# A decoder layer on one core: squares of the inverse square root on ScalarE, narrower shuffles, block sums by additions, masks and decays on GpSimd

## The chip, the core and the metric

The kernel runs on one core of a Trainium2 chip. The metric is the time of one execution on the device in microseconds (us). In the profile, TensorE is PE (PEld for its weight loads), VectorE is DVE, ScalarE is ACT, GpSimd is POOL, and SyncE, which issues the DMAs, is SP.

## What is computed

One decoder layer for a prompt (16 meta tokens and 256 tokens) and eight sample sequences of four tokens: 304 columns in all, 288 once the meta tokens are dropped. The width is 2048. Cut to what matters, the reference is:

```python
z = rms_norm(x, norm_mix) @ w_in
o_a, S_a = rwkv7_mixer(z[..., :RWKV_COLS], ...)   # 16 heads of 64, a recurrence over tokens
o_b, S_b = retention_mixer(z[..., RWKV_COLS:], ...)   # 4 heads of 256, in chunks
h = x + concat(o_a, o_b) @ w_out
hn = rms_norm(h, norm_ffn)
h = h + (silu(hn @ w_gate) * (hn @ w_up)) @ w_down
y = rms_norm(h, norm_final)
```

The places that need 1/sqrt are the three RMS norms, the length of the RWKV keys (`kk / max(sqrt(sum(kk*kk)), 1e-12)`), the group norm behind the RWKV heads, and the RMS norm behind the retention heads. The RWKV recurrence is computed in units of 64 tokens; inside a unit a triangular system has to be inverted.

## The kernel before

**Weights and projections.** All weights come from HBM in one packed stream, in the order in which they are used. `cast` (line 617) has ACT round 512 columns to a short float format (`wh`), and `rest` (line 629) has DVE compute what was cut off (`wl`). Each projection tile is three matmuls per 128 rows of depth (`xh` by `wh`, `xl` by `wh`, `xh` by `wl`) that add into a PSUM bank called `acc`; there are two of these banks. `main` (line 634) issues them one after the other: first 59 tiles of the input projection, in the order of `ORDER` (p: the three tiles k, r, v of a pair of RWKV heads; r: the six tiles q, k, v of a retention head; g: its two gate tiles), then the output projection in two halves, then the FFN.

**Streams.** Everything else runs beside this as generators, called streams: `constants`, `lora_post`, `lora_weights`, `pair` with `by_token`, `inverse`, `units`, `sample`, `bonus` and `pair_out` for each of the eight pairs of heads, and `ret` for each of the four retention heads. A stream issues some instructions for any of the engines and then yields. Its matmuls use six PSUM banks called `mm`.

**The order.** PE runs its instructions strictly in the order of the program, and so does each other engine. The order is found by a planner before the program is made. `Plan.book` (line 348) gives every instruction a price from its engine, its operation and its width, and keeps a clock for each engine, so that the draft knows when each stream's step would be ready. `Plan.pick` (line 426) looks at PE's clock: as long as a stream's step is ready by then, that step is issued, and otherwise the next projection matmul. The draft's choices are then repeated when the real program is made. The prices that bear on this change are, in `book`:

```python
dur, tail = {"stream_shuffle": (148, 90), ...}.get(what, (62 + per * n + 67 * each, 83))
dur, tail = (60 + 0.85 * n, 60) if what == "memset" else (185 + 0.8 * n, 60) if what == "tensor_copy" else (265 + 2 * n, 60)
```

The second line is GpSimd's: 265 + 2 n ns for a product or sum of n columns. An instruction that needs the result of the one before it on the same engine is started `tail` plus 30 ns after that one's duration. The draft also notes how long each tile lives, and `Room` lays the tiles out in one arena from that; in the profile they are all called `arena_dt.float` or `arena_dt.float32r`. A wrapper (line 302) issues every instruction, so all of them carry that line, and a group is known by its shape and tile.

**The pieces that are touched.** `rsqrt` (line 705) computes 1/sqrt on DVE: a scale and an added epsilon (or a floor), a shift and a subtraction of the bits for a first guess, and two corrections, each with two products and an addition. It is called with 304 columns in `constants`, with 312 and a floor in `pair`, with 288 in `pair_out` and in `ret`, and with 3 columns in `rstd_from`, which serves the last two norms. `lora_weights` (line 870) loads two small weight tiles for a pair, twice per pair, and splits them into `hi` (ACT) and `lo` (DVE); in the second call ACT then copies a part of `lo` into `hi`. `inverse` (line 1095) inverts the triangular system: it multiplies `mt` by a mask, sums four 16-column blocks of it into `rr` by a reduction, sends 15 rows of `rr` to all rows of their block by stream shuffles on DVE, in three groups of five, and lets GpSimd do 15 steps of a multiply and an add each on 15 - s columns of five units (75 columns in step 0, 5 in step 14). Then DVE makes two masked copies of `mt`, called `em`, masks the result, transposes it, spreads it over blocks, and PE multiplies. `sample` (line 1219) runs the sample sequences of a pair; it decays the state `s0` by `d4` before it adds what the new tokens bring.

Of the kernel before, what the change touches and what calls it, by code (L numbers as in the profile page):

```python
# [15 lines left out]
P = 128  # L16
# [290 lines left out]
class Plan:  # L307
# [40 lines left out]
    def book(self, eng, what, a, k):  # L348
# [14 lines left out]
        if eng == "PE":  # L363
            done = self.array(what, *a[:3], at) + 170
        elif eng == "SP":
            self.clock[eng] = at = max(self.clock[eng] + 400, at)
            self.dma = max(self.dma, at + 1400) + 4 * out.shape[0] * n / 320
            done = self.dma + 600
        else:
            part = out.shape[0] < P  # L370
            each = sum(math.prod(x.shape[1:]) == 1 for x in ins) if n > 1 else 0
            if eng == "DVE":
                big = max(math.prod(x.shape[1:]) for x in aps)
                per = 0.56 if what == "tensor_scalar" and ins[0].name not in self.banks else 1.05
                dur, tail = {"stream_shuffle": (148, 90), "transpose": (95 + 1.02 * n, 80), "tensor_reduce": (40 + 1.8 * big, 85),
                             "tensor_tensor_scan": (65 + 2.1 * n, 85)}.get(what, (62 + per * n + 67 * each, 83))
            elif eng == "ACT":
                dur, tail = 108 + 0.83 * n + 90 * each - 40 * (ins[0].name in self.banks), 94
            else:
                dur, tail = (60 + 0.85 * n, 60) if what == "memset" else (185 + 0.8 * n, 60) if what == "tensor_copy" else (265 + 2 * n, 60)  # L380
# [158 lines left out]
class Step:  # L539
# [165 lines left out]
    def rsqrt(self, src, scale, eps, floor=None, out=None):  # L705


        dve = self.dve
# [3 lines left out]
        a = self.t([m, n], "rsa")  # L712
        if floor is not None:
            dve.tensor_scalar(x, src, floor, None, op0=ALU.max)
        else:
# [17 lines left out]
    def start(self):  # L733
# [3 lines left out]
        self.dve.memset(self.ones, 1.0)  # L737
        xh, xl = self.xh, self.xl
# [131 lines left out]
    def lora_weights(self, p, half, z):  # L870
# [12 lines left out]
        dve.tensor_sub(lo, lw, hi)  # L883
# [211 lines left out]
    def inverse(self, mt):  # L1095
# [13 lines left out]
        ems = []  # L1109
# [109 lines left out]
    def sample(self, p, v, ax, axd, bs, d4, s0):  # L1219
# [60 lines left out]
        dve.tensor_mul(s0, s0, d4.to_broadcast([P, NB, 64]))  # L1280
# [489 lines left out]
```

## Time and profile before

| | us |
|---|---|
| median of 3 runs | 1557.36 |
| lowest and highest | 1556.4 and 1557.76 |
| the profiled execution | 1558.99 |
| its span, first to last instruction | 1557.1 |
| busy: ACT wh<-wr, 826 casts | 501.6 |
| busy: DVE wl<-wr,wh, 826 subtractions | 563.3 |
| busy: POOL products and sums, 240 | 94.5 |

A row of a group gives line, engine, operation, the tile written and those read, the shape and the count; then the busy time and the mean of one in ns; then the engine's idle time ahead of these instructions and who ended it. A row of a stretch gives the start and end, the length, the busy time and count of PE, PEld, DVE, ACT and POOL, then the granted clock of TensorE, the share of DMA time and GB/s. A row of the order in time gives start, length, engine and operation; neighbours of one operation are merged under the shape of the first, and in brackets stands the idle time before and who ended it. The span and the device time differ by the work around the program, 1.9 us in this execution.

### The profile page before, as it was taken

Reading aid. Unit: us, or ns where it says so; the run is one execution under the profiler, and the core shown is the slowest. Engines: PE = TensorE matmul, PEld = TensorE weight load, DVE = VectorE, ACT = ScalarE, POOL = GpSimd, SP = SyncE. Lnnn points to the kernel's source line nnn. Section 1 sums busy time; section 2 is a strip of 40 time slices with the busy share of each in tenths; the row PEclk is TensorE's granted clock in tenths of the full one; section 3 lists DMA queues with packets and bytes.
Section 4 is the critical chain, followed back from the end, with each engine's and each line's share of the span. In section 5 each row is a group of like instructions: output and inputs, shape, how many; then the busy total and the mean of one; then the engine's idle time right before and its main releaser. Section 6 shows DMA issues by size and latency. Waiting matters only on the chain.

```text
span 1557.1 us, 30803 instructions
## 1 busy us (share of the span) xinstructions
PE 1535.6 (99%) x11388; PEld 1505.7 (97%) x11388; DVE 1102.0 (71%) x2590; ACT 821.4 (53%) x1795; POOL 179.2 (12%) x567
## 2 busy tenths in 40 slices
PE   9999999999999999999999999999999999999997
PEld 8999999998999999999999999999999999999997
DVE  7999888996999786676555565555565656565657
ACT  6766776766676555455444444444444444444445
POOL 0454415513143000000000000000000000000000
PEclk9999999999999999999999999999999999999999
DMA  7443443434545546755555555555555555555553
GB/s 249 154 136 119 127 130 120 115 107 152 181 143 176 170 143 238 243 167 161 164 173 163 174 156 172 162 165 169 168 163 172 164 166 164 171 166 166 161 176 118
DMA packets 76997, 252.48 MB, mean 162 GB/s; under 512 B 9392, under 2 KB 14640, under 8 KB 76848
## 3 DMA queue, kind: packets, MB, share of 16 engines
q1 hardware_dynamic: 76848, 250.52, 51.5%
q8 instruction: 90, 1.47, 0.4%
q14 instruction: 59, 0.48, 0.1%
HBM read 236.21 MB, written 14.28 MB: 161 GB/s over the span
## 4 chain that ended last, share of the span: by engine, by line
PE 85%; DVE 11%; issue 1%; ACT 1%; DMA 1%; POOL 0%; SPq 0%; DVEq 0%; ACTq 0%; POOLq 0%
PE acc L302 76%; PE mm L302 9%; DVE arena_dt.float L302 8%; DVE wl L302 3%; ACT arena_dt.float L302 1%; DMA arena_dt.float<-xT 0%; POOL arena_dt.float L302 0%; DMA arena_dt.float<-lora 0%; ACT wh L302 0%; DVE arena_dt.float32r L302 0%; DMA wr<-big 0%; ACT arena_dt.float32r L302 0%; SPq L302 0%; DVEq L1766 0%; ACT xh L302 0%
## 5 line engine op out<-in xcount | busy, mean ns | idle before, releaser
L302 PE MATMUL acc<-xh,wh 128*128 128x288 f32 (+2 forms) x2592 | 790.9, 305 | 0.0
L302 PE MATMUL acc<-xh,wl 128*128 128x288 f32 (+2 forms) x2592 | 769.9, 297 | 0.9 <-DVE wl L302 0.8
L302 PE MATMUL acc<-xl,wh 128*128 128x288 f32 (+2 forms) x2592 | 766.7, 296 | 0.0
L302 ACT CAST wh<-wr 128x512 fp32r<-128x512 f32 x826 | 501.6, 618 | 373.2 <-PE acc L302 343.3
L302 DVE TENSOR_TENSOR wl<-wr,wh 128x512 fp32r<-128x512 f32 x826 | 563.3, 690 | 114.5 <-ACT wh L302 112.1
L302 PEld LDWEIGHTS acc<-xh,wh 128*128 128x128 f32 x2592 | 487.7, 188 | 4.8 <-issue 1.5
L302 PEld LDWEIGHTS acc<-xl,wh 128*128 128x128 f32 x2592 | 486.9, 188 | 4.0 <-issue 0.7
L302 PEld LDWEIGHTS acc<-xh,wl 128*128 128x128 f32 x2592 | 486.0, 188 | 2.0 <-DVE wl L302 1.5
L302 PE MATMUL acc<-arena_dt.float32r,wh 128*128 128x288 f32 x1408 | 280.0, 294 | 0.4 <-ACT arena_dt.float32r L302 0.3
L302 PEld LDWEIGHTS acc<-arena_dt.float32r,wh 128*128 128x128 f32 x1408 | 225.5, 188 | 0.9 <-ACT arena_dt.float32r L302 0.6
L302 PE MATMUL acc<-arena_dt.float32r,wl 128*128 128x288 f32 x704 | 207.0, 294 | 0.0
L302 DVE TENSOR_TENSOR arena_dt.float<-acc,arena_dt.float 128x288 f32<-128x288 f32 (+4 forms) x181 | 72.7, 420 | 167.6 <-PE acc L302 167.3
L302 PE MATMUL mm<-arena_dt.float 128*128 128x128 f32 (+7 forms) x1072 | 168.4, 317 | 6.2 <-DVE arena_dt.float L302 4.9
L302 DVE TENSOR_TENSOR arena_dt.float<-arena_dt.float 128x288 f32<-128x288 f32 (+11 forms) x483 | 159.5, 354 | 11.7 <-ACT arena_dt.float L302 6.2
L302 DVE TENSOR_TENSOR arena_dt.float<-arena_dt.float,acc 128x288 f32<-128x288 f32 x208 | 94.4, 454 | 100.8 <-PE acc L302 100.6
L302 PEld LDWEIGHTS mm<-arena_dt.float 128*128 128x128 f32 (+1 forms) x1072 | 138.2, 182 | 20.6 <-issue 9.3
L302 ACT ACTIVATE arena_dt.float<-arena_dt.float 128x288 f32<-128x288 f32 (+6 forms) x200 | 85.0, 432 | 119.5 <-DVE arena_dt.float L302 118.2
L302 PEld LDWEIGHTS acc<-arena_dt.float32r,wl 128*128 128x128 f32 x704 | 132.7, 189 | 0.0
L302 ACT COPY arena_dt.float<-mm 64x64 f32<-64x64 f32 (+8 forms) x330 | 91.1, 287 | 72.6 <-PE mm L302 62.4
L302 POOL TENSOR_TENSOR arena_dt.float<-arena_dt.float 128x75 f32<-128x75 f32 (+14 forms) x240 | 94.5, 394 | 100.4 <-DVE arena_dt.float L302 75.6
L302 ACT CAST arena_dt.float32r<-arena_dt.float 128x288 fp32r<-128x288 f32 (+4 forms) x73 | 30.5, 424 | 102.2 <-DVE arena_dt.float L302 89.6
L302 POOL COPY arena_dt.float<-arena_dt.float 128x32 f32<-128x32 f32 (+5 forms) x123 | 35.6, 321 | 125.9 <-DVE arena_dt.float L302 74.0
(64 smaller groups left out, 676.0 us busy)
## 6 DMA issues: line engine op xcount, KB each, us to landing
wr<-big SPq DMA_DIRECT2D x409, 512.0 KB, 3.5
arena_dt.float<-s0r SPq DMA_DIRECT2D x16, 512.0 KB, 6.4
out_rts<-arena_dt.float SPq DMA_DIRECT2D x16, 512.0 KB, 5.4
arena_dt.float<-xT SPq DMA_DIRECT2D x4, 576.0 KB, 6.5
out_y<-arena_dt.float SPq DMA_DIRECT2D x8, 288.0 KB, 2.2
arena_dt.float<-xT SPq DMA_DIRECT2D x7, 304.0 KB, 5.6
wr<-big SPq DMA_DIRECT2D x8, 256.0 KB, 5.3
arena_dt.float<-lora SPq DMA_DIRECT2D x16, 128.0 KB, 3.7
```

The lines of the kernel that those rows point to most:

```text
L302: return self._plan.keep(f(*a, **k))
```

## The change

In `rsqrt`, a call is wide if it has more than 64 columns. A wide call without a floor has ACT scale and add epsilon; for this three columns with epsilons are made in `start` by GpSimd memsets. In both corrections of a wide call ACT squares the guess y, and DVE multiplies the square by x; narrow calls multiply on DVE, in the order x y and then by y. In `lora_weights`, `lo` is computed on GpSimd. In `inverse`, the two `em` masks are made on GpSimd, ahead of the chain of multiplies and adds; the four blocks are summed by two additions (four blocks to two, two to one) in place of the reduction; and a shuffle moves only the columns that the chain reads of it. In `sample`, GpSimd decays `s0`, right after `xs` is copied and not after the transpose. Two of the planner's prices are changed: that of a shuffle, and that of a product or sum on GpSimd.

```diff
@@ Plan.book
-  "stream_shuffle": (148, 90)
+  "stream_shuffle": (62 + 1.05 * n, 90)
-  ... else (265 + 2 * n, 60)
+  ... else (250 + 1.8 * n, 60)
@@ rsqrt
+        wide = n > 64
         if floor is not None:
             dve.tensor_scalar(x, src, floor, None, op0=ALU.max)
+        elif wide:
+            act.activation(x, src, AF.Identity, scale=scale, bias=self.eps[eps][:m])
+            yield
         else:
             dve.tensor_scalar(x, src, scale, eps, op0=ALU.mult, op1=ALU.add)
...
-        dve.tensor_mul(a, x, y)
-        yield
-        dve.scalar_tensor_tensor(a, a, -0.703952253, y, op0=ALU.mult, op1=ALU.mult)
-        dve.scalar_tensor_tensor(y, a, 0.703952253 * 2.38924456, y, op0=ALU.add, op1=ALU.mult)
-        yield
-        dve.scalar_tensor_tensor(a, x, -0.5, y, op0=ALU.mult, op1=ALU.mult)
-        dve.tensor_mul(a, a, y)
-        yield
-        dve.scalar_tensor_tensor(y, a, 1.5, y, op0=ALU.add, op1=ALU.mult)
+        for c, d in (0.703952253, 2.38924456), (0.5, 3.0):
+            if wide:
+                yield
+                act.activation(a, y, AF.Square)
+                yield
+                dve.scalar_tensor_tensor(a, a, -c, x, op0=ALU.mult, op1=ALU.mult)
+            else:
+                dve.tensor_mul(a, x, y)
+                yield
+                dve.scalar_tensor_tensor(a, a, -c, y, op0=ALU.mult, op1=ALU.mult)
+            dve.scalar_tensor_tensor(y, a, c * d, y, op0=ALU.add, op1=ALU.mult)
@@ start
+        self.eps = {}
+        for e in {RMS_EPS, GN_EPS, 4 * RMS_EPS}:
+            self.eps[e] = self.t([P, 1], f"eps{len(self.eps)}", pool=self.cp)
+            self.pool.memset(self.eps[e], e)
@@ lora_weights
-        dve.tensor_sub(lo, lw, hi)
+        self.pool.tensor_sub(lo, lw, hi)
@@ inverse
+        ems = []
+        for li in range(2):
+            em = self.t([P, NU, 64], "em")
+            pool.memset(em[:, NU - 1], 0.0)
+            pool.tensor_mul(em[:, :NU - 1], mt[:, 1:],
+                            cst("lvl", 128)[:, li * 64:(li + 1) * 64][:, None, :].to_broadcast([P, NU - 1, 64]))
+            ems.append(em)
         yield
         rr = self.t([P, NU, 16], "rr")
-        dve.tensor_reduce(rr, rb.rearrange("p u q c -> p u c q"), axis=AX.X, op=ALU.add)
+        dve.tensor_add(rb[:, :, :2], rb[:, :, :2], rb[:, :, 2:])
+        dve.tensor_add(rr, rb[:, :, 0], rb[:, :, 1])
...
-                dve.stream_shuffle(rs[:, s - c[0]], rr, [16 * (i // 16) + s for i in range(32)])
+                dve.stream_shuffle(rs[:, s - c[0], :, s + 1:], rr[:, :, s + 1:],
+                                   [16 * (i // 16) + s for i in range(32)])
...
-        for li in range(2):
-            em = self.t([P, NU, 64], "em")
-            pool.memset(em[:, NU - 1], 0.0)
-            dve.tensor_mul(em[:, :NU - 1], mt[:, 1:],
-                           cst("lvl", 128)[:, li * 64:(li + 1) * 64][:, None, :].to_broadcast([P, NU - 1, 64]))
-            ems.append(em)
-        yield
@@ sample
+        pool.tensor_mul(s0, s0, d4.to_broadcast([P, NB, 64]))
...
-        dve.tensor_mul(s0, s0, d4.to_broadcast([P, NB, 64]))
```

More of the change, by code (lines that the diff above doesn't have):

```diff
@@ L374, in book @@
                 per = 0.56 if what == "tensor_scalar" and ins[0].name not in self.banks else 1.05
-                dur, tail = {"stream_shuffle": (148, 90), "transpose": (95 + 1.02 * n, 80), "tensor_reduce": (40 + 1.8 * big, 85),
+                dur, tail = {"stream_shuffle": (62 + 1.05 * n, 90), "transpose": (95 + 1.02 * n, 80), "tensor_reduce": (40 + 1.8 * big, 85),
                              "tensor_tensor_scan": (65 + 2.1 * n, 85)}.get(what, (62 + per * n + 67 * each, 83))
@@ L379, in book @@
             else:
-                dur, tail = (60 + 0.85 * n, 60) if what == "memset" else (185 + 0.8 * n, 60) if what == "tensor_copy" else (265 + 2 * n, 60)
+                dur, tail = (60 + 0.85 * n, 60) if what == "memset" else (185 + 0.8 * n, 60) if what == "tensor_copy" else (250 + 1.8 * n, 60)
             if part and eng != "POOL":
@@ L705, in rsqrt @@
     def rsqrt(self, src, scale, eps, floor=None, out=None):
-        dve = self.dve
+        dve, act = self.dve, self.act
         m, n = src.shape
@@ L1103, in inverse @@
         pool.tensor_copy(x, cst("i16", 16)[:, None, :].to_broadcast([P, NU, 16]))
+        ems = []
[5 more added lines that the diff above has]
+            ems.append(em)
         yield
         rr = self.t([P, NU, 16], "rr")
-        dve.tensor_reduce(rr, rb.rearrange("p u q c -> p u c q"), axis=AX.X, op=ALU.add)
+        dve.tensor_add(rb[:, :, :2], rb[:, :, :2], rb[:, :, 2:])
+        dve.tensor_add(rr, rb[:, :, 0], rb[:, :, 1])
         yield
         tm = self.t([P, NU, 16], "tm")
-        ems = []
         for c in (0, 5), (5, 10), (10, 15):
```

## The prediction

> **What bounds the kernel now.** I read the page's first and fourth parts, then the busy time by stage, then who ends TensorE's waits.
>
> ```profile
> span 1557.1 us, 30803 instructions
> PE 1535.6 (99%) x11388; PEld 1505.7 (97%) x11388; DVE 1102.0 (71%) x2590; ACT 821.4 (53%) x1795; POOL 179.2 (12%) x567
> PE 85%; DVE 11%; issue 1%; ACT 1%; DMA 1%; POOL 0%; SPq 0%; DVEq 0%; ACTq 0%; POOLq 0%
> ```
> ```profile
> core 0: us, PE busy (x) PEld busy (x) DVE busy (x) ACT busy (x) POOL busy (x), PEclk, DMA share, GB/s
> 65.00:565.00 500.00, 491.74 (x3558) 467.05 (x3556) 437.46 (x1341) 339.92 (x916) 168.92 (x536) 1.00 0.44 137
> 550.00:620.00 70.00, 70.00 (x510) 67.12 (x510) 55.03 (x120) 35.50 (x76) 0.00 (x0) 1.00 0.62 209
> 715.00:1517.00 802.00, 802.00 (x6068) 802.00 (x6067) 470.35 (x839) 339.35 (x593) 0.00 (x0) 1.00 0.55 167
> ```
>
> TensorE (PE) works all the time; the change removes no matmul. After 715 us nothing it touches runs. The stage it works in, from 65 to 565 us, leaves PE idle for 500 - 491.74 = 8.26 us, and that is nearly all there is to win or to add to. VectorE (DVE) is 437.46/500 = 87% busy there. Who ends PE's waits (us in total, times, longest):
>
> ```profile
> PE mm L302 <- DVE arena_dt.float L302: 5.7, 6, 2.4
> PE mm L302 <- ACT arena_dt.float L302: 1.6, 2, 0.9
> PE acc L302 <- DVE wl L302: 0.8, 1, 0.8
> ```
>
> Most of it is DVE, 5.7 + 0.8 = 6.5 us. The largest wait, 2.41 us, has a second bill, shown by four microseconds before and after it and by the same 32 matmuls there and in another head:
>
> ```profile
> 364.00:368.00 4.00, 1.59 (x11) 1.31 (x11) 3.83 (x13) 0.39 (x1) 0.82 (x4) 1.00 0.95 327
> 368.00:372.00 4.00, 4.00 (x41) 2.13 (x39) 2.33 (x6) 2.32 (x7) 0.00 (x0) 0.62 0.95 292
> L302 PE MATMUL mm<-arena_dt.float 128*32 128x256 f32 x32 | 3.6, 627 | 0.0
> L302 PE MATMUL mm<-arena_dt.float 128*32 128x256 f32 x32 | 1.9, 382 | 0.0
> ```
>
> After the idle stretch the granted clock is 0.62, and matmuls that take 1.9 us elsewhere take 3.6: 1.7 us more. The Trainium skill (TensorE: Matmul & The Clock Gate, Part 1) has the clock halve after an idle window of about 3.4 us; here a wait of 2.41 us sufficed, so the trace agrees in kind, and by the page's window a shorter stall would cost no clock either.
>
> DVE's own order of work says why that wait arose:
>
> ```profile
> 361.12 0.78 DVE L302 TENSOR_TENSOR arena_dt.float<-arena_dt.float,cst 128x256 f32<-128x256 f32 x2 [1.01 <-POOL arena_dt.float L302]
> 362.51 1.94 DVE L302 TENSOR_TENSOR arena_dt.float<-arena_dt.float 128x16 f32<-128x16 f32 x9
> 364.48 0.63 DVE L302 TENSOR_TENSOR arena_dt.float<-mm,arena_dt.float 128x448 f32<-128x448 f32 x1
> 365.14 1.40 DVE L302 TENSOR_TENSOR arena_dt.float<-arena_dt.float,cst 128x256 f32<-128x256 f32 x4
> 366.83 0.69 DVE L302 TENSOR_TENSOR arena_dt.float<-arena_dt.float,cst 128x512 f32<-128x512 f32 x1
> 367.67 0.57 PE L302 MATMUL mm<-arena_dt.float 128*128 128x128 f32 x3 [2.41 <-DVE arena_dt.float L302]
> ```
>
> The pair at 361.12 is, by shape and place, the two `em` masks: they stand 1.01 us behind GpSimd (POOL), then take 0.78, and everything after them on DVE, up to the `spread` at 366.83 that releases PE, is that much later.
>
> One thing decides what the rest is worth. The kernel places every step by its own price list, and PE fills a latency that this list knows with projection matmuls. Only time that the list does not know becomes a PE wait.
>
> **Part by part.** Prices first (count, busy us and mean ns of one):
>
> ```profile
> L302 DVE TENSOR_SCALAR arena_dt.float<-mm 128x288 f32<-128x288 f32 x12 | 5.4, 453 | 2.7 <-PE mm L302 2.7
> L302 DVE TENSOR_TENSOR arena_dt.float<-arena_dt.float 128x288 f32<-128x288 f32 x131 | 59.7, 459 | 5.1 <-ACT arena_dt.float L302 2.6
> L302 DVE TENSOR_TENSOR arena_dt.float<-arena_dt.float 128x312 f32<-128x312 f32 x72 | 33.0, 478 | 0.5
> L302 DVE TENSOR_TENSOR arena_dt.float<-arena_dt.float,cst 128x256 f32<-128x256 f32 x24 | 9.3, 431 | 1.1 <-POOL arena_dt.float L302 1.0
> L302 DVE TENSOR_TENSOR arena_dt.float<-arena_dt.float 128x512 f32<-128x512 f32 x8 | 5.5, 682 | 0.1
> L302 DVE TENSOR_TENSOR arena_dt.float32r<-arena_dt.float,arena_dt.float32r 128x256 fp32r<-128x256 f32 x16 | 6.7, 419 | 0.4 <-ACT arena_dt.float32r L302 0.4
> L302 DVE TENSOR_REDUCE arena_dt.float<-arena_dt.float 128x80 f32<-128x320 f32 x8 | 5.7, 714 | 0.0
> L302 DVE TENSOR_TENSOR arena_dt.float<-arena_dt.float,cst 128x160 f32<-128x160 f32 x8 | 2.5, 317 | 0.0
> L302 DVE STREAM_SHUFFLE arena_dt.float<-arena_dt.float 128x80 f32<-128x80 f32 x120 | 20.8, 241 | 0.0
> L302 ACT ACTIVATE arena_dt.float<-mm,half 128x312 f32<-128x312 f32 x16 | 7.4, 516 | 3.0 <-PE mm L302 2.9
> L302 ACT ACTIVATE arena_dt.float<-arena_dt.float 128x288 f32<-128x288 f32 x91 | 40.4, 444 | 95.3 <-DVE arena_dt.float L302 95.2
> ```
> ```profile
> L302 POOL TENSOR_TENSOR arena_dt.float<-arena_dt.float 128x5 f32<-128x5 f32 x1 | 0.2, 208 | 0.1
> L302 POOL TENSOR_TENSOR arena_dt.float<-arena_dt.float 128x75 f32<-128x75 f32 x1 | 0.3, 321 | 11.1 <-DVE arena_dt.float L302 11.1
> L302 POOL TENSOR_TENSOR arena_dt.float<-arena_dt.float 128x75 f32<-128x75 f32 x1 | 0.9, 890 | 0.1
> ```
>
> *rsqrt.* 13 wide calls without a floor (8 in `pair_out`, 4 in `ret`, one in `constants`) lose the scale on DVE and two products: 13 x (453 + 2 x 459) = 17.8 us. 8 calls with a floor lose two products: 8 x 2 x 478 = 7.6 us. ScalarE (ACT) gains 13 x (516 + 2 x 444) + 16 x 444 = 25.4 us. Each wide call now crosses between DVE and ACT four or five times, each time possibly behind a weight cast. The price list knows the crossings, and the last results have cover: from 550 to 620 us, where the last heads finish, PE is busy 70.00 of 70.00. Without it a call would cost about the ACT time put into its chain, 1.4 us, less the 1.4 us of DVE work taken out, plus its crossings. Where the list is wrong by a cast, PE waits that much; I add 0.3 us, from ACT's load rising by 25.4/339.92 = 7% on its 1.6 us. Narrow calls (both ends of the FFN) keep nine instructions: nothing. Three memsets at the start run on an idle POOL.
>
> *Masks, `s0`, `lo`.* Off DVE: 16 x 431 = 6.9, 8 x 682 = 5.5, 16 x 419 = 6.7, together 19.1 us. On POOL nothing so wide is in the trace. From the rows of 5 and 75 columns the slope is (321 - 208)/70 = 1.6 ns, so 256 columns take 0.61 and 512 columns 1.02 us (an estimate): 32 x 0.61 + 8 x 1.02 = 27.7 us. The third row is the upper side: the next multiply of the same shape and chain, with DVE now in two-input work, took 890, 2.8 times as long; so between 27.7 and 78 us. I take about 42, 1.5 times, as most instructions meet less. POOL stays under half busy. New waits: the ACT copy of `lo` into `hi` (weight casts queue behind it), the lora matmuls behind `lo`, and, behind `s0` and the masks on POOL, its copies and the chain. `lo` can find a third of a chain ahead of it, 14.2/3 = 4.7 us by the sum row below; the list knows POOL's queue, so only its error there, a third of a microsecond, would reach the casts. `s0` is wanted only by the last addition of `sample`, many steps later; if that cover were gone each would cost its 1.02 us. No DMA is moved; their queue on SyncE stays as it is.
>
> *Reduce and shuffles.* 5.7 us becomes two adds, at most 8 x 2 x 317 = 5.1 and, with the second half as wide, nearer 4.5: 1.2 us saved. The 120 shuffles go from 80 to 40 columns on average: between nothing (all fixed cost) and half of 20.8; I take 5. Their price in the list falls with the width too; if the cost is fixed, that is one more thing it under-prices, by at most 10 us of DVE time over the whole stage.
>
> DVE's sum is 25.4 + 19.1 + 1.2 + 5 = 51 us, 12% of 437.46 (44 to 57).
>
> *The GpSimd chain.* Its eight runs in `inverse` (30 multiplies and adds each), POOL's busy time in the first, the shortest and the last, and their sum:
>
> ```profile
> 79.74:95.08 15.34, 13.06 (x31) 1.00 0.46 138
> 440.70:453.20 12.50, 10.31 (x33) 1.00 0.68 256
> 492.04:506.81 14.77, 12.50 (x31) 1.00 0.62 205
> sum 113.61, POOL 95.58; mean POOL 11.95
> ```
>
> On average 113.61/8 = 14.2 us. The old list gives 30 x 265 + 2 x 1200 columns + 30 x 90 between dependent steps = 13.05; the new one, with 250 and 1.8, 12.36. (Behind the eight chains, in windows of 5 to 10 us each, PE idles 54.70 - 51.06 = 3.64 us in all, 2.41 of it at one place; behind some, as at 190 us, nothing:
>
> ```profile
> 189.70:195.00 5.30, 5.30 (x44) 1.00 0.54 173
> sum 54.70, PE 51.06; mean PE 6.38
> ```
>
> so I let half of what a chain is late reach PE.) The work is the same, so the list's error grows from 1.15 to 1.84 us if the chain keeps its length. With two-input work off DVE it may shorten: I take 13.8, an error of 1.4, 0.25 more on eight chains, half of it felt: +1.0 us. The masks ahead of it, 2 x 0.61 us, run beside DVE's product with `m16`, its adds and five shuffles, some 3 x 0.32 + 5 x 0.17 = 1.8 us by the rows of 160 and 80 columns: the chain does not start later unless POOL is held.
>
> **Sum.** At 364 us the masks' 1.01 + 0.78 go, so the 2.41 becomes about 0.7 (-1.7), too short for the clock to drop (-1.7). The other DVE-ended waits, 6.5 - 2.4 = 4.1, shrink by a quarter, about twice DVE's 12%: -1.0. Against it +1.0 (chain) and +0.3 (ACT). Total -3.1: a span of 1554.0. The profiled execution took 1558.99, 1.9 more than its span and 1.6 more than the median of 1557.36; against the median I forecast **1554.3**.
>
> **Rivals.** *Waits only move (1556 to 1559).* The list knows that DVE is lighter and places PE's steps earlier, so PE comes as early as before to what is mis-priced. And the list does not hold that POOL and DVE stop each other, as the row of 890 shows: if DVE stands still for the 27.7 us of new wide work on POOL, its relief is 51 - 28 = 23 us, and the change hardly does what it says. Then half of the 364 us site's gain is left (-1.7) and of the other DVE waits a tenth (-0.4), against +1.0 and +0.3: 1556.6, or 1558.3 if nothing of that site is won. The Trainium skill (SBUF — State Buffer, Who interferes with whom) makes this a rule against the change: a GpSimd instruction and a DVE instruction with two SBUF inputs take a shared port in turn, each blocked for the other's whole length. The 890 agrees with it for POOL's side; how long DVE is held, these rows do not show. Against this rival: ScalarE's share of the relief, 25 us, is free of it.
>
> *All DVE-ended waits go:* -6.5 and -1.7 of clock, at 1549.2. For it: DVE at (437 - 51)/500 = 77%. Against: the chains' error stays.
>
> *Slower: the chain priced too short (1562).* If the chains stay at 14.2 us, each is later than planned by 1.84 - 1.15 = 0.69 us more; felt in full, eight times, that is 5.5 us, and one new stall of over two microseconds adds 1.7 of clock and ACT 0.3. Half of the 364 us site's gain (-1.7) and the other DVE waits (-1.0) stand against it: +4.8. It decides once DVE's relief right behind a chain is under 0.69 us. For it: the largest PE wait now stands behind a chain. Against: behind some chains PE does not wait at all.
>
> **Chances.** Forecast (1552 to 1556) 0.42, on both sides of the 0.2%, 3.1 us, which is about what a measurement here can tell from no change: 0.27 faster, 0.15 same. Waits only move 0.22, same. All go 0.15, faster. Slower 0.21, of which 0.20 beyond the bound. So 0.42 faster, 0.38 same, 0.20 slower. The range takes in the full relief and the slow chain: 1548.5 to 1562.
>
> **What would show it.** From 65 to 565 us DVE falls to 385 to 400 us, ACT rises to about 365, POOL to 195 to 215; PE idles 5 to 6 us; no stretch has a clock near 0.6; 128x256 DVE work with a constant falls from 24 to 8. Wrong: DVE above 415 (blocking), chains of over 14.5 us with PE waits behind them, ACT-ended PE waits over 3 us, or a new stall of over 2 us.

## The result, and the profile after

| | before | after |
|---|---|---|
| median on the same chip, 4 runs each | 1556.88 us | 1579.3 us |
| lowest and highest | 1555.43 to 1557.76 | 1575.78 to 1581.51 |
| ratio, 95% interval | | 1.0143 (1.0122 to 1.0163) |

The changed kernel is 22 us slower, 1.4%. The profiled execution took 1579.41 us, with a span of 1577.6. The first and the fourth part of the page of the changed kernel:

```profile
span 1577.6 us, 30797 instructions
...
PE 1545.5 (98%) x11388; PEld 1513.4 (96%) x11388; DVE 1073.3 (68%) x2503; ACT 842.5 (53%) x1850; POOL 210.2 (13%) x610
...
PE 80%; DVE 10%; DMA 2%; ACT 2%; POOL 2%; issue 2%; SPq 0%; DVEq 0%; POOLq 0%; ACTq 0%
```

The engines did what the change says: DVE's busy time falls by 28.7 us, ACT's and POOL's rise by 21.1 and 31.0. PE does the same 11,388 matmuls. The busy time by stretch shows that it waits more (columns as in the prediction: start and end, length, PE, PEld, DVE, ACT, POOL, granted clock, DMA share, GB/s):

```profile
65.00:565.00 500.00, 483.15 (x3459) 459.04 (x3457) 401.08 (x1239) 346.35 (x932) 196.83 (x569) 0.99 0.43 135
...
85.00:105.00 20.00, 17.96 (x124) 17.71 (x123) 14.35 (x46) 8.81 (x20) 10.28 (x35) 0.91 0.47 147
...
265.00:285.00 20.00, 16.94 (x113) 16.70 (x112) 16.71 (x42) 7.72 (x15) 14.63 (x36) 0.91 0.44 134
...
365.00:385.00 20.00, 18.22 (x127) 17.79 (x126) 11.30 (x33) 10.97 (x29) 7.66 (x26) 0.91 0.37 125
```

From 65 to 565 us PE idles 16.85 us, where it idled 8.26. Three stretches of 20 us lack 2.04, 3.06 and 1.78 us of PE time, and in each the clock was 0.91 on average: 9% of 20 us, about 1.8 us more. Those three together are 6.9 + 5.4 = 12.3 us. Who ended PE's idle time there, from the order of PE's instructions in time:

```profile
94.96 0.43 PE L302 MATMUL acc<-xh,wl 128*128 128x304 f32 x1 [2.04 <-DVE wl L302]
...
275.01 0.40 PE L302 MATMUL acc<-xh,wl 128*128 128x290 f32 x1 [3.06 <-DVE wl L302]
...
374.43 0.41 PE L302 MATMUL acc<-xh,wl 128*128 128x304 f32 x1 [1.78 <-DVE wl L302]
```

In all three a projection matmul waits for `wl`, the remainder of a weight tile that DVE computes. These matmuls are what PE fills its time with while the heads are late, so now the filler itself is late. DVE's order in time says why, with one row of GpSimd's order below it:

```profile
93.58 0.73 DVE L302 TENSOR_TENSOR arena_dt.float<-arena_dt.float,cst 128x160 f32<-128x160 f32 x2 [4.62 <-POOL arena_dt.float L302]
...
273.11 0.72 DVE L302 TENSOR_TENSOR arena_dt.float<-arena_dt.float,cst 128x160 f32<-128x160 f32 x2 [3.15 <-POOL arena_dt.float L302]
273.75 1.21 DVE L302 TENSOR_TENSOR wl<-wr,wh 128x512 fp32r<-128x512 f32 x1
...
372.46 0.76 DVE L302 TENSOR_TENSOR arena_dt.float<-arena_dt.float,cst 128x160 f32<-128x160 f32 x2 [4.63 <-POOL arena_dt.float L302]
...
258.65 14.43 POOL L302 TENSOR_TENSOR arena_dt.float<-arena_dt.float 128x75 f32<-128x75 f32 x30 [3.57 <-DVE arena_dt.float L302]
```

The product of 160 columns with a constant is `xm` in `inverse`, the first thing that reads the chain's result. GpSimd's chain ends at 258.65 + 14.43 = 273.08, and `xm` starts at 273.11. DVE, which works strictly in order, has stood in front of it for 3.15 us. `wl` is next in its order, and PE resumes at 275.01, just behind it. The waits by line, first of before (one row that was not shown), then of after:

```profile
DVE arena_dt.float L302 <- POOL arena_dt.float L302: 1.2, 2, 1.0
```
```profile
DVE arena_dt.float L302 <- POOL arena_dt.float L302: 26.5, 8, 4.6
...
PE acc L302 <- DVE wl L302: 8.0, 5, 3.1
...
PE mm L302 <- DVE arena_dt.float L302: 6.6, 10, 1.7
...
PE mm L302 <- DMA arena_dt.float<-s0r: 1.2, 2, 0.6
```

DVE waits for GpSimd 26.5 us, eight times, once per pair of heads, up to 4.6 us; before it was 1.2. PE's waits for `wl` rise from 0.8 to 8.0.

**Where this comes from.** The diff shows it, in lines that read as the mere move of the masks: the block that made `em` behind the chain ended in a `yield`, and that went with the block.

```diff
                 pool.tensor_add(x[:, :, s + 1:], x[:, :, s + 1:], tm[:, :, s + 1:])
-        for li in range(2):
...
-            ems.append(em)
-        yield
         xm = self.t([P, NU, 32], "xm")
```

A stream's step is issued as a whole. So `xm` now goes into DVE's queue in the same step as the last ten instructions of the chain go into GpSimd's, and DVE stands at it until they are done: 1.3 to 4.6 us in each of the eight pairs. The planner can put other DVE work behind a step, but not into it.

**The rest of the span.** The chain of waits shows one long run of 6066 uninterrupted matmuls in both kernels (start, length), in a part of the program that the change doesn't touch. First before, then after:

```profile
714.41 802.10 PE acc L302 x6066
```
```profile
731.03 805.46 PE acc L302 x6066
```

The changed kernel reaches this run 16.6 us later. PE's idle time makes 10.2 of that, 8.6 us from 65 to 565 us and 1.6 after it. Lower clock makes about 1.7: ahead of the run there are three stretches of it against two, as before has one at its start too (from 5 to 25 us its clock is 0.91). Some 4.7 us are left, in which PE is busy longer with the same matmuls; these rows don't assign them. The run itself took 3.4 us longer, with PE busy throughout at a clock of 1.00; more on that at the end.

### The profile page after: what moved, and what is told of

It reads as the page before. It is cut to its first block, busy times and chain, and to the rows that moved or that the text cites. A ratio compares the mean times of both kernels' runs of the same rounds, so it can differ in the third digit from the quotient of the medians.

```text
span 1577.6 us, 30797 instructions
## 1 busy us (share of the span) xinstructions
PE 1545.5 (98%) x11388; PEld 1513.4 (96%) x11388; DVE 1073.3 (68%) x2503; ACT 842.5 (53%) x1850; POOL 210.2 (13%) x610
## 4 chain that ended last, share of the span: by engine, by line
PE 80%; DVE 10%; DMA 2%; ACT 2%; POOL 2%; issue 2%; SPq 0%; DVEq 0%; POOLq 0%; ACTq 0%
PE acc L302 73%; PE mm L302 8%; DVE arena_dt.float L302 8%; DVE wl L302 3%; POOL arena_dt.float L302 2%; ACT arena_dt.float L302 2%; DMA arena_dt.float<-s0r 1%; DMA arena_dt.float<-xT 1%; ACT wh L302 1%; DMA wr<-big 0%; DMA out_rts<-arena_dt.float 0%; SPq L302 0%; DVE arena_dt.float32r L302 0%; ACT arena_dt.float32r L302 0%; POOLq L302 0%
## 5 line engine op out<-in xcount | busy, mean ns | idle before, releaser
L302 ACT ACTIVATE arena_dt.float<-arena_dt.float 128x288 f32<-128x288 f32 (+6 forms) x242 | 103.3, 435 | 131.4 <-DVE arena_dt.float L302 130.0
L302 DVE TENSOR_TENSOR arena_dt.float<-arena_dt.float 128x32 f32<-128x32 f32 (+12 forms) x449 | 151.6, 362 | 8.8 <-ACT arena_dt.float L302 4.5
L302 ACT COPY arena_dt.float<-mm 64x64 f32<-64x64 f32 (+7 forms) x330 | 91.4, 286 | 70.9 <-PE mm L302 63.7
L302 POOL TENSOR_TENSOR arena_dt.float<-arena_dt.float 128x70 f32<-128x70 f32 (+15 forms) x248 | 98.5, 397 | 50.4 <-DVE arena_dt.float L302 24.9
L302 DVE TENSOR_TENSOR arena_dt.float<-arena_dt.float,cst 128x320 f32<-128x320 f32 (+4 forms) x52 | 25.3, 505 | 36.0 <-POOL arena_dt.float L302 26.5
```

Source lines behind the costliest of these rows:

```text
L302: return self._plan.keep(f(*a, **k))
```

## The experiments

Two theories at first. **A, the lost yield:** putting it back restores the time. **B, GpSimd's wide products** (`em`, `s0`, `lo`), which stop DVE's two-input instructions. Beside them stood the new prices, and the square roots on ScalarE. Ratios are to the kernel before, in the same session on the same chip, with 95% intervals; before had medians of 1557.6 to 1558.4 us in them.

**1. The yield back into the changed kernel.**

```diff
+        yield
         xm = self.t([P, NU, 32], "xm")
```

> The changed kernel with one yield put back in inverse, between the last ten multiplies and adds on GpSimd and the DVE product xm that reads their result. Theory (the lost yield): the change took the yield behind the em masks away with them, so xm is now issued in the same step as the last third of the GpSimd chain and DVE stands at it, with the weights' wl behind it. Expected: DVE's wait for GpSimd ahead of the 128x160 product falls from 26.5 us to under 4, PE's wait for wl from 8.0 to about 1, time 1552 to 1560. Rival (prices too low): those are as in the changed kernel, so 1573 to 1582. Rival (GpSimd holds DVE's port, or the crossings to ScalarE): the wide GpSimd work and the crossings are all there, so over 1570.

Measured: 1570.02 us, 1.0073 (1.0058 to 1.0088). Some 9 us came back, less than half. The waits of this kernel:

```profile
PE mm L302 <- DVE arena_dt.float L302: 14.7, 13, 2.1
...
DVE arena_dt.float L302 <- POOL arena_dt.float L302: 5.0, 4, 1.9
```

DVE's wait for GpSimd falls from 26.5 to 5.0 us, and PE's wait at a projection matmul for `wl` is gone, as A says. But the waits of the small matmuls (`mm`) for DVE rise from 6.6 to 14.7 us, so something else is there too. PE's idle time from 65 to 565 us is 17.3 us, no less than the changed kernel's 16.9:

```profile
65.00:565.00 500.00, 482.69 (x3481) 459.85 (x3480) 410.68 (x1247) 352.15 (x949) 193.85 (x569) 0.99 0.43 134
```

So run 1 shows that the waits moved, and the 9 us can't be read off them. Of the 8.8 us between the two spans, 2.7 are the long run of matmuls, which took 802.73 us here. One place of the new waits in the order in time:

```profile
242.38 1.04 POOL L302 TENSOR_TENSOR arena_dt.float<-arena_dt.float,cst 128x256 f32<-128x256 f32 x1 [4.85 <-ACT arena_dt.float L302]
243.46 0.80 POOL L302 TENSOR_TENSOR arena_dt.float<-arena_dt.float,cst 128x256 f32<-128x256 f32 x1
243.59 2.44 DVE L302 TENSOR_TENSOR arena_dt.float<-arena_dt.float 128x64 f32<-128x64 f32 x6
...
244.22 1.04 POOL L302 TENSOR_TENSOR arena_dt.float<-arena_dt.float 128x512 f32<-128x512 f32 x1
...
249.75 0.51 PE L302 MATMUL mm<-arena_dt.float,cst 128*128 128x320 f32 x1 [2.06 <-DVE arena_dt.float L302]
```

Two masks and `s0` run on GpSimd without a break from 242.38 to 245.26. Beside them DVE does the small products of `sample` that the matmul of 320 columns at 249.75 needs, and that matmul waits 2.06 us. The groups of DVE from 243.3 to 245.3 us in the same kernel, with a row of before for the usual time of one:

```profile
L302 DVE TENSOR_TENSOR arena_dt.float<-arena_dt.float 128x48 f32<-128x48 f32 x1 | 1.1, 1064 | 0.0
L302 DVE TENSOR_SCALAR arena_dt.float<-arena_dt.float 128x288 int32<-128x288 int32 x1 | 0.9, 927 | 0.0
L302 DVE TENSOR_TENSOR arena_dt.float<-arena_dt.float 128x64 f32<-128x64 f32 x1 | 0.7, 749 | 0.0
```
```profile
L302 DVE TENSOR_SCALAR arena_dt.float<-arena_dt.float 128x288 int32<-128x288 int32 x24 | 7.4, 309 | 0.9
```

A product of 48 columns takes 1064 ns here, as long as the 1.04 us of the GpSimd product beside it. Against the means of the same operations in before (221, 309 and 236 ns) the three together took 2.0 us longer, about as much as the matmul waits. That is B, to be tested by itself.

**2 to 4. The same yield taken out of before; the old prices in the changed kernel; its square roots back on DVE.**

```diff
-        yield                       (before, behind the em block)
```
```diff
-  "stream_shuffle": (62 + 1.05 * n, 90) ... (250 + 1.8 * n, 60)
+  "stream_shuffle": (148, 90) ... (265 + 2 * n, 60)
```
```diff
-        wide = n > 64
+        wide = False
```

> The kernel before with nothing changed but that one yield taken out of inverse (the masks stay on DVE, ahead of xm). Theory (the lost yield): DVE waits for GpSimd in front of the masks or xm for 15 to 30 us in all (1.2 before), PE's wait for wl rises to over 5, time 1568 to 1580. Rivals (prices, port, crossings): none of them is in this kernel, so 1555 to 1560.

> The changed kernel with the planner's old prices (shuffle 148, GpSimd 265 + 2 n). Theory (the lost yield): DVE still waits for GpSimd for 20 us or more in front of xm, time 1572 to 1583. Rival (the chain priced too short, the slower case of the prediction): the planner comes later to what follows the chain, so under 1563.

> The changed kernel with every rsqrt on DVE alone (no call is wide). Theory (the lost yield): the waits in front of xm stay at 20 us or more, time 1573 to 1584, as DVE has 25 us more to do. Rival (crossings between DVE and ScalarE): the crossings are gone, so under 1565.

Measured: 1600.76 us, 1.0276 (1.0259 to 1.0293); 1602.31, 1.0286 (1.0264 to 1.0307); 1619.85, 1.0397 (1.0381 to 1.0412). All three are far slower than either theory says, so something that none of the edits is about had changed. It was in the plan's arena. `Room` lays out the tiles so that between the last use of a tile and the first of the next one in the same bytes there is a gap; it tries several gaps and orders, and keeps the layout that lacks least. For these three kernels it found a layout only with a gap of nothing: over all tiles, 753.6 us are missing to the 0.8 us that it wants behind each, against 286 for before, 4.9 for the changed kernel and 0 for run 1. These are the planner's own figures. With no gap, a step would have to wait wherever the tile before it in the same bytes is late; where that happened was not followed up. So I gave `Room` a second try, called the loose layout below: with a gap of one microsecond, a tile that finds no place moves ahead in the order in which tiles are placed.

```diff
+            for _ in range(60):
+                found = self.pack(order, limit, 1000.0)
+                if not isinstance(found, int):
+                    best = found if best is None or found[0] < best[0] else best
+                    break
+                j = order.index(found)
+                order.insert(j // 2, order.pop(j))
```

All runs that follow have it.

**5 and 6. Before, and before without the yield, in the loose layout.**

> The kernel before with the same order of instructions, its tiles only laid out anew: where the packer finds no place for a tile it moves that tile ahead and tries again, so that nearly every tile keeps the 0.8 us between one use of its memory and the next that the packer aims at (missing in all 4 us; 286 us over 942 tiles in the layout before). Theory (tight layouts make waits of their own): somewhat faster, 1549 to 1556. Rival (the layout does not matter): 1556 to 1560.

> The kernel before without the yield behind the masks, as in e2, but laid out loosely (missing 9 us in all; in e2 the packer had found no place but at no distance at all, 754 us). Theory (the lost yield, and most of e2's 43 us from its layout): 1564 to 1578, with DVE's waits for GpSimd at 15 us or more. If the layout is nothing: as e2, 1595 to 1603. If the yield is nothing: 1549 to 1560.

Measured: 1560.37 us, 1.0018 (1.0008 to 1.0027), and 1566.79, 1.0057 (1.0042 to 1.0072). The gain that run 5 was to bring by its roomier layout did not come. Run 6 has the edit of run 2, in the same order of instructions, and is 34 us faster: that much of run 2 was the layout. With nothing but the yield taken out, before is 6.4 us slower (run 6 against run 5), and PE idles 13.3 us in place of 7.1 from 65 to 565 us. PE's waits in run 6 show it at the place that A names (0.7 us in run 5):

```profile
PE acc L302 <- DVE wl L302: 4.7, 5, 1.5
```

DVE's waits for GpSimd were 9.5 us in all, less than expected; why they are shorter in this plan was not followed up.

**7. Masks and `s0` back on DVE, where they were, with the yield.** The rest of the change stays (the square roots on ACT, the additions, the narrow shuffles, `lo` on GpSimd, the prices).

```diff
-            pool.tensor_mul(em[:, :NU - 1], ...)   (ahead of the chain)
+            dve.tensor_mul(em[:, :NU - 1], ...)    (behind it, then yield)
-        pool.tensor_mul(s0, s0, d4.to_broadcast([P, NB, 64]))
+        dve.tensor_mul(s0, s0, d4.to_broadcast([P, NB, 64]))   (where it was)
```

> The changed kernel with the yield back as in e1 and with the masks and the decay of s0 on DVE again, where they stood before; laid out loosely (missing 5 us). Theory (wide GpSimd products stop DVE's products with two inputs, and PE waits at the 128x320 matmul of sample that needs them): those five waits, 9 us in e1, fall under 2 us; time 1552 to 1560. Rival (the extra 12 us of e1 come from ScalarE's squares or the prices): 1566 or more.

Measured: 1559.06 us in 10 runs, 1.0009 (1.0 to 1.0019). That is before again, within what can be told apart. PE's waits for DVE at the small matmuls fall to 3.1 us. What the rest of the change costs or brings is too small to be told here.

**8. The square roots back on DVE in the changed kernel, loose layout.** The edit is that of run 4.

> The changed kernel with every rsqrt on DVE as in e4, laid out loosely (missing 7 us; in e4 754 us). Theory (e4's 40 us over the changed kernel came from its layout): 1576 to 1592, DVE's extra 25 us costing at most some 10. If the layout is nothing: 1615 to 1623. Rival (the crossings to ScalarE cost time): under 1570.

Measured: 1581.0 us, 1.0148 (1.0131 to 1.0165), 39 us below run 4 and as slow as the changed kernel. So the squares on ScalarE show no part in the loss, and no gain is seen to go with them either, as far as two different plans can tell (runs 16 to 18).

**9 and 10. Only one of the two back on DVE** (with the yield): `s0` on DVE and the masks on GpSimd; then the masks on DVE and `s0` on GpSimd. The edits are the halves of run 7's.

> As p5 (yield back, 1559.1 us), but with the masks on GpSimd and only the decay of s0 on DVE. Theory (wide GpSimd products stop DVE): the masks are the longer and come ahead of rb and the products of sample, so most of the 11 us between p5 and e1 come back: 1563 to 1569. If s0 alone were to blame: under 1561.

> As p5, but with the decay of s0 on GpSimd and only the masks on DVE. Theory: s0 goes out right ahead of DVE's products of sample in the same step, so each pair may pay up to its 1.0 us: 1560 to 1567. If the masks alone were to blame: under 1561.

Measured: 1563.43 us, 1.0037 (1.0022 to 1.0052), and 1557.79 in 10 runs, 1.0001 (0.9991 to 1.0010). The masks on GpSimd cost some 4 to 6 us. `s0` alone costs nothing that can be told, where 1560 to 1567 was expected: it is one product of a microsecond per pair, where the masks are two, ahead of the chain and beside `sample`'s products.

**11 and 12. Is it the time on GpSimd, or what GpSimd does in it?** Both are run 7 with extra GpSimd work that nobody reads, at the places of the masks and of `s0`: memsets of about that length in one, the same products written to scratch in the other.

```diff
+            pool.memset(ds, 0.0)                     (896 columns, twice; 640 columns, twice)
```
```diff
+            pool.tensor_mul(ds, mt[:, 1:], cst("lvl", 128)...)
+        pool.tensor_mul(ds, s0, d4.to_broadcast([P, NB, 64]))
```

> p5 plus GpSimd memsets of scratch tiles, as long as the masks (two of 896 columns) and the s0 product (two of 640), at the places where the changed kernel has those; masks and s0 stay on DVE, nothing reads the scratch. It tells apart whether GpSimd being busy costs the time, or GpSimd reading two tensors beside DVE. Theory (DVE's two-input work is stopped by a GpSimd product that reads SBUF): memsets read nothing, so 1557 to 1562, and DVE's 48-column products stay near 0.2 us. Rival (the chain starts later behind them): 1565 to 1573, as p9.

> p5 plus the same three GpSimd products as in the changed kernel, written to scratch tiles that nothing reads; masks and s0 stay on DVE. Theory: DVE products of 16 to 64 columns beside them take 0.7 to 1.1 us in place of 0.2, and PE waits at the 128x320 matmul again: 1566 to 1574, while p8 stays at p5's time. If they cost nothing: 1557 to 1561, and the 11 us between p5 and e1 are not from the products as such.

Measured: 1560.65 us in 10 runs, 1.0015 (1.0005 to 1.0025), with the memsets; 1569.33, 1.0076 (1.0061 to 1.0091), with the products. This is the cleanest comparison of the study. DVE does the same work in all three kernels and GpSimd is busy for about as long in the last two, yet only the products cost, 10 us over run 7. Groups of run 7, then of the memsets, then of the products:

```profile
L302 DVE TENSOR_TENSOR arena_dt.float<-arena_dt.float 128x48 f32<-128x48 f32 x48 | 10.2, 213 | 0.4
```
```profile
L302 DVE TENSOR_TENSOR arena_dt.float<-arena_dt.float 128x48 f32<-128x48 f32 x48 | 10.4, 218 | 0.4
...
L302 POOL MEMSET arena_dt.float<- 128x896 f32 x16 | 13.1, 846 | 0.1
...
L302 POOL MEMSET arena_dt.float<- 128x640 f32 x16 | 10.4, 652 | 0.5
```
```profile
L302 DVE TENSOR_TENSOR arena_dt.float<-arena_dt.float 128x48 f32<-128x48 f32 x48 | 15.8, 328 | 0.4
...
L302 POOL TENSOR_TENSOR arena_dt.float<-arena_dt.float,cst 128x256 f32<-128x256 f32 x16 | 14.7, 938 | 36.0 <-ACT arena_dt.float L302 31.8 <-DVE arena_dt.float L302 4.1
...
L302 POOL TENSOR_TENSOR arena_dt.float<-arena_dt.float 128x512 f32<-128x512 f32 x8 | 8.6, 1069 | 0.0
```

The products of 48 columns take 213, 218 and 328 ns on average. On the whole of DVE that is little; it hurts because it falls on the step that a matmul waits for. PE's waits for DVE at the small matmuls, in the kernel with the scratch products:

```profile
PE mm L302 <- DVE arena_dt.float L302: 13.5, 13, 1.8
```

They were 3.1 us in run 7 and 4.8 with the memsets. The 10.4 us more than in run 7 cover the difference, which is 8.9 us between the two profiled spans and 10.3 between the medians. At the 128x320 matmul of `sample` alone, PE's waits for DVE sum to 9.2 us with the products, 1.7 with the memsets and 0.4 in run 7. The Trainium skill (SBUF — State Buffer, Who interferes with whom) has both halves of this: a DVE instruction with two inputs in SBUF contends with a GpSimd instruction that reads SBUF, not with one that only writes it. The three means agree.

**13. The yield out again, with masks and `s0` on DVE.** Run 7 without its yield.

> p5 (masks and s0 on DVE, yield back) without the yield. If the two causes add up, the yield costs here what it costs between e1 and the changed kernel (9.3 us) or between the two kernels before (6.4): 1564 to 1570. If the yield only hurts together with the wide GpSimd products: under 1562.

Measured: 1562.8 us, 1.0031 (1.0019 to 1.0043). The yield is worth 3.7 us here, less than the 1564 to 1570 that was expected if the two causes add up, and PE idles 10.2 us in place of 5.7 from 65 to 565 us. Its waits:

```profile
DVE arena_dt.float L302 <- POOL arena_dt.float L302: 20.2, 8, 3.1
...
PE acc L302 <- DVE wl L302: 4.9, 6, 1.5
```

The eight waits of DVE are back, and PE's for `wl`. None of PE's six is over 1.5 us in this plan, where the changed kernel has one of 3.1.

**14. The old prices in the changed kernel, loose layout.** The edit of run 3.

> The changed kernel with the planner's old prices as in e3, but laid out loosely (missing 3 us; 754 in e3). Theory (prices have no part): 1574 to 1585, near the changed kernel's 1579.3. Rival (the new prices place steps too early behind the chain): under 1572. If the layout is nothing: 1598 to 1606.

Measured: 1569.06 us, 1.0074 (1.0059 to 1.0090): missed, as it is 10 us faster than the changed kernel, where the rival had put it. (It is 33 us faster than run 3: that was the layout again.) Either the new prices had caused part of the loss, or another plan of the same work differs by that much.

**15. A candidate.** Run 10 with `lo` on DVE as well, so that of the moved products GpSimd keeps only `s0`:

```diff
-        self.pool.tensor_sub(lo, lw, hi)
+        dve.tensor_sub(lo, lw, hi)
```

> p7 (yield back, masks on DVE, s0 on GpSimd; 1557.8 us) with lo on DVE too. Theory (a GpSimd product stops DVE whichever it is): lo's sixteen products held DVE for 5 us in p7, at places with little waiting on them, so 1555 to 1559. If lo was worth leaving on GpSimd: over 1560.

Measured: 1557.95 us in 11 runs, 1.0004 (0.9995 to 1.0013). It doesn't beat before.

**16 to 18. Prices, or plans?** The changed kernel with GpSimd's price at 252 + 1.8 n in place of 250 + 1.8 n; with the old GpSimd price alone; and with both old prices and the yield.

```diff
-  (250 + 1.8 * n, 60)
+  (252 + 1.8 * n, 60)
```

> The changed kernel with the planner's price for a GpSimd product at 252 + 1.8 n in place of 250 + 1.8 n, laid out loosely. If a re-plan alone moves the time by several us (so that p11 says little of the prices): it lands anywhere from 1568 to 1584, 3 us or more from 1579.3. If plans close to each other give the same time: 1577 to 1582.

> The changed kernel with the old GpSimd price alone (265 + 2 n), laid out loosely. If the GpSimd price, too low for the chain, is the third cause: near p11, 1566 to 1572. If it is the shuffle's price or chance: 1574 to 1584.

> e1 (yield back, 1570.0 us) with both old prices, laid out loosely. If the prices are a cause of their own: 4 us or more under e1, 1558 to 1566. If they only matter where DVE stands at xm, or by chance: 1567 to 1573.

Measured: 1570.89 us, 1.0086 (1.0071 to 1.0102); 1572.63, 1.0098 (1.0081 to 1.0115); 1564.46, 1.0045 (1.0030 to 1.0060). Run 16 differs from the changed kernel by two nanoseconds in a price and by the loose layout, and in no work at all, and it is 8 us faster. With nearly the new prices it is 1.8 us from run 14, so run 14's 10 us say nothing of the prices: the scatter of plans is about as large, and a single difference of some microseconds between two plans isn't evidence of a cause. Run 17 lies between its two ranges. Run 18 is 5.5 us under run 1, in the range that was to mean that the prices are a cause of their own; but it is one such difference, so with the yield in, a part of the prices is neither shown nor excluded. What stands is what holds across plans:

| | masks and `s0` on GpSimd | on DVE |
|---|---|---|
| no yield | 1569.1, 1570.9, 1572.6, 1579.3, 1581.0 | 1562.8, 1566.8 |
| yield | 1564.5, 1570.0 | 1559.1, and before: 1557 to 1560.4 |

(The 1569.3 of run 12 has both sets of products, and belongs beside the 1570.0. Runs 9, 10 and 15, with a part on each engine, took 1563.4, 1557.8 and 1558.0.) By the means, in each column the yield is faster, and in each row DVE is; single times overlap, as 1569.1 without the yield and 1570.0 with it. By the means of the cells, the yield is worth some 6 to 7 us, and the place of the masks and `s0` some 8 to 10.

The places of the waits tell the two causes apart in every plan, and better than the times do (us; the second column is summed from PE's order in time):

| | PE for `wl` | PE for DVE at the 128x320 matmul |
|---|---|---|
| yield, products on DVE: before, runs 5 and 7 | 0.5 to 0.8 | 0 to 0.4 |
| no yield, products on DVE: runs 6 and 13 | 4.7 and 4.9 | 0 and 0.5 |
| yield, products on GpSimd: runs 1, 12 (scratch) and 18 | 0 | 8.3, 9.2 and 3.3 |
| no yield, products on GpSimd: the changed kernel, runs 8, 14, 16 and 17 | 4.6 to 8.0 | 4.1 to 5.6 |

The wait for `wl` comes and goes with the yield, the wait at the 128x320 matmul with the masks and `s0` on GpSimd (runs 9, 10 and 15, with a part, lie between, at 3.3, 2.0 and 1.2 us). In the changed kernel they are 8.0 and 4.1 us.

## Why the prediction was wrong

**The step that failed** is the list of what the moved masks leave behind. The prediction counted the masks as work taken off DVE behind the chain, and named what would be queued at each new wait: "the ACT copy of `lo` into `hi`", the lora matmuls, and GpSimd's own copies and chain. It left out that the block ended a step. With it went the only point at which other DVE work could go between the chain's issue and `xm`, so a new wait stood at the head of DVE, with `wl` behind it and the projection matmuls behind that. The forecast took DVE's lighter load as fewer waits (-1.7, -1.7 and -1.0). Instead DVE waited 25.3 us more for GpSimd, and three PE stalls with their clock cost 12.3 us. Runs 1, 6 and 13 show these waits come and go with the yield alone changed.

**The second failure** is how the stop of DVE by GpSimd was priced. The rival "Waits only move" named the mechanism, and spread its 28 us over the whole stage as a relief that shrinks: 1556.6 to 1558.3. Runs 11 and 12 show that 23 us of products on GpSimd cost 9 to 10 us, since they fall on one short run of DVE products with a matmul at its end. In the changed kernel that matmul waited 4.1 us for DVE, in before not at all. Here the mechanism was right, and its price was taken from the wrong place: an average over 500 us instead of the step that waits.

**The steps one by one.** DVE from 65 to 565 us came to 401.08 us, just above the 385 to 400 expected (with 99 fewer matmuls' worth of work in the window, so the relief is a little overstated by it). POOL's 196.83 lies in the range given. ACT's 346.35 stays below the 365; PE's waits for its small tiles fell from 1.6 to 0.9 us, and those for its casts `wh` rose from 1.2 to 2.3: +0.4 together, where +0.3 was added. The DVE products of 256 columns with a constant fell from 24 to 8, as listed. PE was to idle 5 to 6 us and idled 16.85. Groups of the changed kernel for the prices:

```profile
L302 POOL TENSOR_TENSOR arena_dt.float<-arena_dt.float,cst 128x256 f32<-128x256 f32 x16 | 14.1, 880 | 28.6 <-ACT arena_dt.float L302 28.6
...
L302 POOL TENSOR_TENSOR arena_dt.float32r<-arena_dt.float,arena_dt.float32r 128x256 fp32r<-128x256 f32 x16 | 14.3, 892 | 91.4 <-ACT arena_dt.float32r L302 78.4 <-issue 13.0
...
L302 POOL TENSOR_TENSOR arena_dt.float<-arena_dt.float 128x512 f32<-128x512 f32 x8 | 9.3, 1165 | 0.0
...
L302 DVE STREAM_SHUFFLE arena_dt.float<-arena_dt.float 128x75 f32<-128x75 f32 (+14 forms) x120 | 16.0, 205 | 0.0
```

The wide GpSimd work took 14.1 + 14.3 + 9.3 = 37.7 us, where 42 was taken between bounds of 27.7 and 78. The shuffles fell from 20.8 to 16.0 us, 4.8 against 5. The eight chains sum to 108.45 us, 13.6 on average, against 14.2 in before and the 13.8 that was taken; the longest, shown above, took 14.43, inside the 14.5 given as the limit:

```profile
sum 108.45, POOL 90.43; mean POOL 11.30
```

So the list's error is 13.6 - 12.36 = 1.2 us, about the 1.15 of before, and there was no ground for the chain's +1.0. The rival that ended slower, 1562 through chains that are priced too short, has the sign but not the mechanism: the chain is no later than it was; what changed is who is queued behind it. The "new stall of over 2 us" among the signs of error is what the profile shows, at `wl`.

**The gain that didn't come.** Where the yield is in and the masks are on DVE (runs 7, 10 and 15), DVE is 18 to 21 us lighter than before from 65 to 565 us, and the time is that of before. The waits that the prediction wanted to shorten were a few microseconds to begin with, and a new plan brings its own. How the 22 us divide between the yield, the products and the scatter of plans stays open beyond the table above, since the parts differ from plan to plan. Whether a wide product could be put on GpSimd at a place where DVE has no two-input work was not tried.

## What to carry to other kernels

When a block is moved in a program whose order is made of steps, look at the step boundary that moves with it: what is now issued together, which in-order queue the first reader of a slow chain stands in, and who is behind it. GpSimd products that read SBUF aren't free space beside a busy DVE; price them at the DVE instructions that run beside them, and at the wait that ends with those, not as a share of a stage. Where a planner re-plans everything, measure its scatter with an edit that means nothing before a difference of some microseconds is given a cause.

## What the runs showed of the hardware

- DVE's held instructions were not only those with two inputs. In run 1 a one-input integer operation of 288 columns took 927 ns beside GpSimd's products, where 309 is its mean before. The Trainium skill (SBUF — State Buffer, Who interferes with whom) counts this kind of operation among those that can take the shared port, and this row agrees. With memsets on GpSimd in place of products, which left the two-input products alone (218 ns against 213), one such operation took 1.92 us (run 11):

```profile
428.06 1.92 DVE L302 TENSOR_SCALAR arena_dt.float<-arena_dt.float 128x288 int32<-128x288 int32 x1
428.19 3.05 POOL L302 MEMSET arena_dt.float<- 128x896 f32 x4
```

- A wait of 1.78 us could lower PE's clock, and one of 2.08 us could leave it. The three waits of 1.78, 2.04 and 3.06 us each left 0.91 in their 20 us, about 1.8 us of time for each, whatever their length; behind the one of 2.04 the clock was 0.50 for at least 3.2 us. In run 16 the wait of 2.08 us at 94.54 left 1.00 in the 20 us around it. First a row of the changed kernel, then two of run 16:

```profile
95.30:98.50 3.20, 3.20 (x15) 3.20 (x14) 3.17 (x10) 0.95 (x2) 0.00 (x0) 0.50 0.74 184
```
```profile
94.54 0.41 PE L302 MATMUL acc<-xh,wl 128*128 128x304 f32 x1 [2.08 <-DVE wl L302]
...
85.00:105.00 20.00, 17.47 (x128) 16.88 (x128) 16.22 (x50) 8.89 (x19) 10.91 (x34) 1.00 0.43 141
```

  The idle window of about 3.4 us that the Trainium skill (TensorE: Matmul & The Clock Gate, Part 1) states is thus not the shortest wait that lowers the clock, and the length of a wait alone doesn't decide; what does stays open.
- The run of 6066 matmuls without a pause, the same in every kernel, took 802.1 to 806.3 us across the profiles of this study, with PE busy all the time. It makes 3.4 of the 20.5 us between the two spans. In runs 7 and 15 it started 4.1 and 6.2 us earlier than in before's profile and took 3.3 and 3.4 us longer, so that part of a small gain ahead of it was not seen in the time. Each kernel has one profile only; whether the plan or the run sets this rate was not tried.
